# A hybrid decoder step on one core: tensors in the chip's layout, state updates by row strips, two selection rounds a stage, and a later landing time for gathers in the emission clock

## The chip, the cores and the metric

The kernel runs on one core of a Trainium2 chip. The metric is the device time of one launch in microseconds (us). All engines of the core take part: TensorE (PE, its weight loads PEld), VectorE (DVE), ScalarE (ACT), GpSimd (POOL) and SyncE (SP), which issues most of the DMAs.

## What is computed

One inference step of a one-layer hybrid trunk, for a prompt of 256 tokens and 8 sequences of 4 new tokens each (32 tokens), 288 token columns together. The core of the reference:

```python
m = silu(c) @ w_ada + b_ada                     # shift, scale, gate
h = rmsnorm(x, g_norm) * (1 + scale) + shift
(u_a, v_a, z_a, qkv_b, z_b, a_b, b_b, q_c, k_c, v_c, z_c, qi_c, ki_c, wi_c) = split(h @ w_in)
y_a = chunk_mlp(gelu(u_a), layernorm(gelu(v_a))) * silu(z_a)          # a_ws: 128x128 causal mixing
q, k, v = silu(causal_conv(qkv_b, conv_prev, dn_conv_w))              # 4 taps, state_conv
o_b, s_new = gated_delta(l2norm(q), l2norm(k), v, g, beta, state_dn)  # 16 heads of 128x128 states
y_b = rmsnorm(o_b, dn_onorm) * silu(z_b)
idx = top_k(indexer scores, 256 of 2052 keys)                         # 8 sequences, paged caches
y_c = attend(q_c, k[idx], v[idx]) * silu(z_c)
x = x + gate * (concat(y_a, y_b, y_c) @ w_out);  y = rmsnorm(x, g_final)
```

The outputs are y, the new keys, values and index keys, the new delta states, the last pre-convolution rows, and v_a of the new tokens. All data are float32; the large matmuls split each operand into a rounded high part and a low part and use three products.

## The kernel before

**Two kinds of work on PE.** The large matmuls (tile `acc`, 128x288 outputs) are 14304 instructions: unit by unit, one unit being two slices of 128 rows of a weight block, four output tiles and three products each (24 instructions a pair, 12 a slice). For each slice ACT rounds the weights (`wh<-w`), DVE forms the low part (`wl<-w,wh`); four such splits are kept ahead (`N_SPLIT`, line 40). Between these units PE does the small steps of the chains: indexer, top-k selection, sparse attention over gathered keys, convolution, the delta rule (`dn_all`, line 1700), the gMLP part.

**The order is written by an emission clock.** All instructions are recorded in one pass in Python. The class `Weaver` keeps a model time for each engine (`W.t`), adds a table cost for each instruction (`cost`, `note`, `note_dma`), and at each step of the large matmuls asks which chain may go on: `stages` (line 237) steps a generator when its data are ready by the model at PE's model time, and stops where the model's DVE or ACT are over 2 us (`BACKLOG`) ahead of PE. Each `yield` ends a stage of a chain. `bank(n)` waits for n of the four small PSUM banks. So the costs in the table decide where in PE's order a chain step stands, and the engines then run their queues strictly in that order. A DMA's landing in the model is its issue, 0.6 us, its bytes at 360 GB/s, and 2.0 us (line 206); for a DMA issued by POOL (key "G", the gathers) 1.0 us of issue comes on top.

**Forced ends.** `finish` steps named chains to their end at once, with no large matmuls between. Three matter here. Before the last unit of the q columns of head group 2 `end_prev` (line 2285) finishes `DN[0]`, the delta chain of head group 0, and before that of group 3 `DN[1]`. `gmlp_open` (line 2144) finishes `DN[3]`. In counts of large matmuls these places lie at 7752, 8904 and 10992 of the 14304.

**The parts that are touched.**
- Small vectors: `load_rows` and `prep_rows` (line 668) load `b_ada`, `g_norm`, `dn_conv_w` as rows and transpose them on PE (`ldT`, 4 steps); the conditioning vectors `C` are loaded as 72 rows, and transposed (`cT`).
- Convolution: `prev_gen` (line 1589) loads 24 rows of the old convolution state for each of 12 column blocks (`prev`), transposes them (`prevT`, 4 matmuls) and copies them (`scT`). `tail_gen` (line 1631) transposes the new last rows (`tailT`, 4 matmuls), copies them (`tailo`) and stores them with two DMAs.
- Delta states of the 8 sequences: `load_states` (line 1966) and `update` (line 2084) move 512 KB a head, in pieces of 512 B. `update` multiplies, for each head of a group, the keys of that head, which stand on 32 of 128 rows of `kgm` with zeros on the others, with `vk` (tile `Sup`, 128 rows x 512 columns, float32; 8 a group, 32 in all). DVE adds four 128x128 parts of each to the state (`St`).
- Selection: `topk_gen` (line 1350) has 32 rounds on DVE (`MAX8`, `MATCH_REPLACE8` over 544 columns), each a stage of its own, with a copy of the eight found values on POOL (`LDn`).
- Sparse attention of the 32 new tokens: `sample_gen` (line 1432), in two halves of four sequences. In each half two lanes take 16 gathers of keys (`kraw`, 512 KB; transposed as `kT`, multiplied as `S`), the selection's mask is applied, and 16 gathers of values (`vraw`) feed the products `so`. The delta chain of group 0 starts when the second half is done.
- gMLP: `gmlp_prep` (line 2155) loads `a_ws` and transposes it (`wmT`, 8 matmuls).

All instructions bear line 74 in the profile, that of the recording helper; tiles tell them apart.

Of the kernel before, what the change touches and what calls it, by code (L numbers as in the profile page):

```python
# [14 lines left out]
OP = mybir.AluOpType  # L15
# [75 lines left out]
class Weaver:  # L91
# [98 lines left out]
    def note_dma(self, key, out, ins):  # L190
# [15 lines left out]
        self.used(self.parts, out, e + 2.0, "D")  # L206
# [174 lines left out]
def tile_hybrid_step(ctx: ExitStack, tc: tile.TileContext, I, O):  # L381
# [50 lines left out]
    bT = const([P, 96], "bT")  # L432
    gnT = const([P, 32], "gnT")
    cwT = const([P, 4, 48], "cwT")
    onT = const([P, 1], "onT")
# [203 lines left out]
    LD = []  # L639

    def load_rows(dst, src, n):
        t = tl("xp", [P, P], "ld", 4)
        G.dma_start(t[:n], src)
        LD.append((dst, t, n))

    cw = I["dn_conv_w"][0].rearrange("j (c p) -> (j c) p", p=P)
    cwv = cwT.rearrange("p j c -> p (j c)")
    load_rows(bT, I["b_ada"][0].rearrange("(c p) -> c p", p=P), 96)
    load_rows(gnT, I["g_norm"][0].rearrange("(c p) -> c p", p=P), 32)
    load_rows(cwv[:, 0:96], cw[0:96], 96)  # L650
    load_rows(cwv[:, 96:192], cw[96:192], 96)
    G.dma_start(onT, I["dn_onorm"].rearrange("o p -> p o"))

    W.take()
    pc = pr4("cT")
    for h in range(2):
        th = tl("xp", [72, 256], "cth", 1)
        ch = C[:, 256 * h:256 * h + 256]
        A.activation(th, ch, AF.Tanh, scale=0.5)
        V.scalar_tensor_tensor(ch, th, 1.0, ch, op0=OP.add, op1=OP.mult)  # L660
    for c in range(4):
        T.transpose(pc[:, c, 0:72], C[:, c * P:(c + 1) * P], ident[0:72, 0:72])
    A.activation(cT[:, 0:KT * 9].rearrange("p (s c r) -> p c r s", c=4, r=9),
                 pc[:, :, 0:72].rearrange("p c (r s) -> p c r s", s=8), AF.Copy, scale=0.5)
    free()
    load_x(1)

    def prep_rows():
        for dst, t, n in LD:
            yield from bank()  # L670
            ps = pr("ldT")
            T.transpose(ps[:, :n], t[:n, :], ident[:n, :n])
            yield
            V.tensor_copy(dst, ps[:, :n])
            free()
        V.tensor_scalar(onT, onT, 0.5, None, op0=OP.mult)
        yield
# [672 lines left out]
    def topk_gen():  # L1350
# [16 lines left out]
        for n in range(32):  # L1367
            mx = LU[:, 31 - n]
            V.max(out=mx, in_=cur)
            if n < 31:  # L1370
                V.match_replace(out=W1, in_to_replace=mx, in_values=cur, imm_value=-3e38)
            G.tensor_copy(LD_[:, n], mx)
            cur = W1
            yield
# [209 lines left out]
    sconv = I["state_conv"][0].rearrange("b r c -> (b r) c")  # L1584
# [4 lines left out]
    def prev_gen(kind, g):  # L1589
        c0 = kind * 2048 + g * 512  # L1590
        prev = u2k("prev")
        dma2(prev[0:24], sconv[:, c0:c0 + 512])
        yield [prev]
        yield from bank()
        ps = pr4("prevT")
        for j in range(4):
            T.transpose(ps[:, j, 0:24], prev[0:24, j * P:(j + 1) * P], ident[0:24, 0:24])
        yield
        CV[kind, g] = scT = tl("dnq", [P, 4, 24], "scT", 2)
        A.copy(scT, ps[:, :, 0:24])  # L1600
        free()
        yield
# [28 lines left out]
    def tail_gen(kind, g, tail):  # L1631
        c0 = kind * 2048 + g * 512
        yield from bank()
        ps = pr4("tailT")
        for c in range(4):
            T.transpose(ps[0:27, c], tail[:, c], ident)
        yield
        to = u2k("tailo")
        A.copy(to[0:27], ps[0:27].rearrange("p c n -> p (c n)"))
        free()  # L1640
        yield
        dma(O[6][0, 0][:, c0:c0 + 512], to[0:3])
        dma(O[11][0].rearrange("b r c -> (b r) c")[:, c0:c0 + 512], to[3:27])
# [322 lines left out]
    def load_states(g, St):  # L1966
        for hl in range(4):
            yield from W.calm()
            dma2(St[hl], I["state_dn"][0][:, 4 * g + hl].rearrange("b d e -> d b e"))

    def dn_sample(g, b):
# [6 lines left out]
        kgm, vn1, os_, junk = yf(0, 4, P), yf(4, P), yf(5, P), yf(7, P)  # L1978
# [26 lines left out]
        G.memset(kgm, 0.0)  # L2005
# [78 lines left out]
        def update():  # L2084
# [3 lines left out]
            for hl in range(4):  # L2088
                for b0 in (0, 4):
                    yield from bank()  # L2090
# [3 lines left out]
                    for b in range(b0, b0 + 4):  # L2094
                        i = 8 * hl + b
                        V.scalar_tensor_tensor(St[hl][:, b], St[hl][:, b], gl[:, i:i + 1],
                                               pu[:, (b - b0) * P:(b - b0 + 1) * P], op0=OP.mult, op1=OP.add)
                    free()
                yield from W.calm()
                dma(O[10][0, :, 4 * g + hl].rearrange("b d e -> d b e"), St[hl])  # L2100
# [382 lines left out]
```

## Time and profile before

| | |
|---|---|
| median of three runs | 2627.51 us (2625.67 to 2632.01) |
| the profiled execution | 2626.0 us, of which the span from first to last instruction is 2624.3 us |
| busy: PE, PEld | 2509.4 us (96%), 2245.5 us (86%) |
| busy: DVE, ACT, POOL | 1625.4 us (62%), 1065.7 us (41%), 496.1 us (19%) |
| mean granted TensorE clock | 0.986 |
| DMA | 615.9 MB, 235 GB/s over the span |

PE is the engine that sets the time: it is busy nearly always, and a matmul's recorded duration includes the wait in its pipeline, so that what a step costs is read from start to start. "Granted clock" is the share of full speed that TensorE was given; 0.50 is 1.2 GHz, 1.00 is 2.4 GHz.

### The profile page before, as it was taken

What the parts mean: (1) busy time and instruction counts of PE and PEld (TensorE: products, weight loads), DVE (VectorE), ACT (ScalarE), POOL (GpSimd) and SP (SyncE); (2) the same over time, 40 slices, a digit from 0 to 9 for tenths busy, and PEclk for the clock granted to TensorE, in tenths of its full rate; (3) what the DMA queues carried; (4) which work ended last, traced back from release to release, by engine and by line L of the source; (5) the groups of instructions that cost most, each with busy time, mean ns of one, the idle gap of its engine ahead of it and who ended that gap; (6) DMA issues with size and microseconds to landing.
All of it is one profiled execution on the core that took longest, in us unless ns stands there. A gap on an engine that the chain in (4) does not pass through costs nothing.

```text
span 2624.3 us, 52262 instructions
## 1 busy us (share of the span) xinstructions
PE 2509.4 (96%) x19684; PEld 2245.5 (86%) x19684; DVE 1625.4 (62%) x3633; ACT 1065.7 (41%) x2440; POOL 496.1 (19%) x1137
## 2 busy tenths in 40 slices
PE   5999999999998999999999989999999999999997
PEld 3788888888897888878789969989989989999997
DVE  3477765555578786744458567568576667555554
ACT  4423223333344443334354434444444544444443
POOL 2000000000001232353543343343430210000000
PEclk9999999999999999999999999999999999999998
DMA  7999988888665567677777547577568455655565
GB/s 285 365 336 342 338 318 323 310 318 302 206 197 182 186 225 251 220 274 236 246 238 238 176 154 234 184 216 245 184 203 265 146 195 187 187 180 174 174 188 164
DMA packets 234964, 615.91 MB, mean 235 GB/s; under 512 B 38856, under 2 KB 92348, under 8 KB 234712
## 3 DMA queue, kind: packets, MB, share of 16 engines
q1 hardware_dynamic: 223672, 574.65, 64.7%
q0 software_dynamic: 11040, 37.92, 4.3%
q8 instruction: 155, 2.54, 0.4%
q14 instruction: 97, 0.79, 0.1%
HBM read 587.54 MB, written 24.95 MB: 233 GB/s over the span
## 4 chain that ended last, share of the span: by engine, by line
PE 85%; DMA 7%; DVE 3%; POOL 2%; issue 2%; ACT 1%; SPq 0%; ACTq 0%; DVEq 0%; POOLq 0%
PE acc L74 68%; PE ada L74 7%; DMA kraw<-in_cache_k_dram,ixk 2%; DMA wa<-in_w_ada_t_dram 1%; DMA vraw<-in_cache_v_dram,ixv 1%; PE kT L74 1%; DMA w<-in_w_in_t_dram 1%; PE Sup L74 1%; DVE wl L74 1%; PE YP L74 1%; PE v L74 1%; PE gram L74 1%; PE o L74 1%; POOL vraw L74 1%; PE S L74 1%
## 5 line engine op out<-in xcount | busy, mean ns | idle before, releaser
L74 DVE TENSOR_TENSOR wl<-w,wh 128x512 fp32r<-128x512 f32 (+1 forms) x1216 | 802.2, 681 | 687.4 <-ACT wh L74 680.8
L74 ACT CAST wh<-w 128x512 fp32r<-128x512 f32 (+1 forms) x1216 | 715.0, 611 | 1145.5 <-PE acc L74 860.0
L74 PE MATMUL acc<-hH,wh 128*128 128x288 f32 (+1 forms) x3744 | 1157.7, 309 | 21.0 <-ACT hH L74 8.7
L74 PE MATMUL acc<-hH,wl 128*128 128x288 f32 (+1 forms) x3744 | 1110.2, 297 | 2.0 <-DVE wl L74 1.9
L74 PE MATMUL acc<-hL,wh 128*128 128x288 f32 (+1 forms) x3744 | 1110.7, 297 | 0.5 <-DVE hL L74 0.5
L74 PEld LDWEIGHTS acc<-hH,wh 128*128 128x128 f32 (+1 forms) x3744 | 708.8, 189 | 132.5 <-issue 57.6
L74 PEld LDWEIGHTS acc<-hH,wl 128*128 128x128 f32 (+1 forms) x3744 | 709.2, 189 | 4.8 <-DVE wl L74 4.4
L74 PEld LDWEIGHTS acc<-hL,wh 128*128 128x128 f32 (+1 forms) x3744 | 710.1, 190 | 3.6 <-issue 2.4
L74 PE MATMUL acc<-mL,wh 128*128 128x288 f32 x1024 | 301.8, 295 | 2.4 <-DVE mL L74 2.4
L74 PE MATMUL acc<-mH,wh 128*128 128x288 f32 x1024 | 303.5, 296 | 0.0
L74 PE MATMUL acc<-mH,wl 128*128 128x288 f32 x1024 | 302.1, 295 | 0.0
L74 PEld LDWEIGHTS acc<-mL,wh 128*128 128x128 f32 x1024 | 192.2, 188 | 2.7 <-DVE mL L74 2.7
L74 PEld LDWEIGHTS acc<-mH,wh 128*128 128x128 f32 x1024 | 192.2, 188 | 0.2
L74 PEld LDWEIGHTS acc<-mH,wl 128*128 128x128 f32 x1024 | 192.2, 188 | 0.0
L74 PE MATMUL ada<-wa,cT 128*32 128x512 f32 x1024 | 135.7, 605 | 15.8 <-DMA wa<-in_w_ada_t_dram 15.5
L74 DVE TENSOR_TENSOR zb<-zb,acc 128x288 f32<-128x288 f32 x160 | 70.3, 451 | 41.4 <-PE acc L74 41.2
L74 POOL TENSOR_TENSOR htmp<-yT,gaT 128x32 f32<-128x32 f32 x20 | 7.8, 388 | 449.2 <-ACT wh L74 335.4
L74 PEld LDWEIGHTS ada<-wa,cT 128*32 128x32 f32 x1024 | 28.2, 109 | 72.9 <-issue 54.7
L74 POOL TENSOR_SCALAR frs<-frs 128x1 f32<-128x1 f32 (+1 forms) x3 | 0.9, 297 | 448.2 <-DVE frs L74 448.0
L74 DVE TENSOR_TENSOR R<-R,R 128x248 f32<-128x248 f32 (+30 forms) x248 | 72.4, 292 | 11.6 <-DMA R<-dD 5.0
L74 POOL TENSOR_SCALAR tap<-xp,cwT 128x32 f32<-128x32 f32 x144 | 78.5, 545 | 0.2
L74 POOL DMA_INDIRECT vraw<-in_cache_v_dram,ixv x64 | 66.9, 1045 | 31.7 <-issue 12.4
(462 smaller groups left out, 2395.4 us busy)
## 6 DMA issues: line engine op xcount, KB each, us to landing
w<-in_w_in_t_dram SPq DMA_DIRECT2D x464, 512.0 KB
wa<-in_w_ada_t_dram SPq DMA_DIRECT2D x256, 512.0 KB
w<-in_w_ada_t_dram SPq DMA_DIRECT2D x128, 512.0 KB
w<-in_w_out_t_dram SPq DMA_DIRECT2D x128, 512.0 KB
St<-in_state_dn_dram SPq DMA_DIRECT2D x16, 512.0 KB
out_dram<-St SPq DMA_DIRECT2D x16, 512.0 KB
X<-in_x_prompt_dram SPq DMA_DIRECT2D x8, 512.0 KB
XF<-in_x_prompt_dram SPq DMA_DIRECT2D x16, 256.0 KB
```

Source lines behind the costliest of these rows:

```text
L74: r = f(*a, **k)
```

## The change

Inputs and outputs get other layouts in DRAM (`lay_out` and a new `put_back`, on the host): the conditioning vectors, the small vectors (one tile `vecs` instead of four), the convolution state, its new rows, the delta states and `a_ws` come and go as the engines use them. So the transposes `cT`, `ldT`, `prevT`, `tailT` and `wmT` and their copies go (112 matmul entries on PE in the order, 24 copies on ACT), the new convolution rows leave with one DMA a block instead of two, and each partition's part of a delta state is 4 KB in one piece. The update of the states takes the keys of a head from its own 32 rows, two heads side by side, each with a bank. Gathers land 4.0 us instead of 2.0 us after their bytes in the emission clock. The selection has two rounds in a stage, and its copies are on ACT.

```diff
-        self.used(self.parts, out, e + 2.0, "D")
+        self.used(self.parts, out, e + (4.0 if key == "G" else 2.0), "D")
...
-    C = tl("xp", [72, 512], "C")
-    dma(C[0:8], I["c_prompt"].rearrange("r (s c) -> (r s) c", c=512))
-    dma(C[8:72], I["c_sample"].rearrange("r (s c) -> (r s) c", c=512))
+    C = tl("xp", [P, KT * 9], "C")
+    dma(C, I["c_t"])
...
+    dma(vecs, I["vecs_t"])
...
     def prep_rows():
-        for dst, t, n in LD:
...
-            T.transpose(ps[:, :n], t[:n, :], ident[:n, :n])
...
+        yield [vecs]
...
-            G.tensor_copy(LD_[:, n], mx)
+            A.copy(LD_[:, n], mx)
             cur = W1
-            yield
+            if n % 2:
+                yield
...
     def prev_gen(kind, g):
-        c0 = kind * 2048 + g * 512
-        prev = u2k("prev")
-        dma2(prev[0:24], sconv[:, c0:c0 + 512])
-        yield [prev]
...
-            T.transpose(ps[:, j, 0:24], prev[0:24, j * P:(j + 1) * P], ident[0:24, 0:24])
...
+        dma2(scT, I["state_conv_t"][4 * kind + g])
+        yield [scT]
...
     def tail_gen(kind, g, tail):
...
-            T.transpose(ps[0:27, c], tail[:, c], ident)
...
-        dma(O[6][0, 0][:, c0:c0 + 512], to[0:3])
-        dma(O[11][0].rearrange("b r c -> (b r) c")[:, c0:c0 + 512], to[3:27])
+        dma(O[6][4 * kind + g], tail)
+        yield
...
-            dma2(St[hl], I["state_dn"][0][:, 4 * g + hl].rearrange("b d e -> d b e"))
+            dma2(St[hl], I["state_dn_t"][4 * g + hl])
...
-        G.memset(kgm, 0.0)
...
-        for hl in range(4):
-            q = slice(32 * hl, 32 * hl + 32)
-            V.tensor_scalar(kgm[q, hl], pa[q, 1], sc[q, 2:3], None, op0=OP.mult)
+        V.tensor_scalar(kg, pa[:, 1], sc[:, 2:3], None, op0=OP.mult)
...
-            for hl in range(4):
+            for h0 in (0, 2):
                 for b0 in (0, 4):
-                    yield from bank()
-                    pu = pr("Sup")
-                    T.matmul(pu, kgm[:, hl], vk[:, b0:b0 + 4].rearrange("p c n -> p (c n)"), start=True, stop=True)
+                    yield from bank(2)
+                    pus = []
+                    for hl in (h0, h0 + 1):
+                        pus.append(pr("Sup"))
+                        q = slice(32 * hl, 32 * hl + 32)
+                        T.matmul(pus[-1], kg[q], vk[q, b0:b0 + 4].rearrange("p c n -> p (c n)"), start=True, stop=True,
+                                 tile_position=(32 * hl, 0))
                     yield
...
     def gmlp_prep():
-        wraw = tl("gm", [P, 8, P], "wraw", 1)
-        dma(wraw, I["a_ws"][0].rearrange("h t s -> t h s"))
+        wmT = tl("gm", [P, 8, P], "wmT", 1)
+        dma(wmT, I["a_ws_t"])
...
-                T.transpose(ps[:, c], wraw[:, 4 * h4 + c], ident)
```

The order moves from the first selection round on. On DVE, at the start of the selection rounds, before the change (`MAX` and `MATCH_REPLACE` are a round, `wl` a weight split, `ktk` the copy of transposed keys):

```order
L74 MAX LU<-SC 128x8
L74 MATCH_REPLACE W_11002<-LU,SC 128x544
L74 TENSOR_TENSOR wl<-w,wh 128x512
L74 MAX LU<-W_11002 128x8
L74 MATCH_REPLACE W_11002<-LU,W_11002 128x544
L74 TENSOR_TENSOR wl<-w,wh 128x512
L74 COPY ktk<-kT 128x512
L74 MAX LU<-W_11002 128x8
L74 MATCH_REPLACE W_11002<-LU,W_11002 128x544
L74 TENSOR_TENSOR wl<-w,wh 128x512
```

And in the changed kernel, at the same place:

```order
L74 MAX LU<-SC 128x8
L74 MATCH_REPLACE W_10918<-LU,SC 128x544
L74 MAX LU<-W_10918 128x8
L74 MATCH_REPLACE W_10918<-LU,W_10918 128x544
L74 TENSOR_TENSOR wl<-w,wh 128x512 x2
L74 MAX LU<-W_10918 128x8
L74 MATCH_REPLACE W_10918<-LU,W_10918 128x544
L74 MAX LU<-W_10918 128x8
L74 MATCH_REPLACE W_10918<-LU,W_10918 128x544
L74 TENSOR_TENSOR wl<-w,wh 128x512
L74 COPY ktk<-kT 128x512
```

Two rounds now stand together, and from the first to the last of the 32 rounds DVE has 35 splits and 7 copies of keys between them, where it had 42 and 14.

On PE, at the forced end of the delta chain of group 0 (7752 large matmuls into the order), before the change (`osm` and `oTs` are the chain's last steps ahead of the update, `kbT`, `gram` and `qkT` belong to the next group):

```order
L74 MATMUL osm<-R_18134,R_18132 128x128
L74 MATMUL oTs<-ident,R_18134 128x128
L74 MATMUL qkT<-ident,cv 128x128 x8
L74 MATMUL Sup<-R_18396,R_18134 128x512 x3
L74 MATMUL kbT<-ident,R_18379 128x128 x2
L74 MATMUL kbT<-ident,R_18381 128x128 x2
L74 MATMUL gram<-R_18379,cv 128x128
```

And in the changed kernel, from `osm` to the first update:

```order
L74 MATMUL osm<-R_17892,R_17890 128x128
L74 MATMUL acc_17337<-hH_8112,wh 128x288
L74 MATMUL acc_17337<-hL_8126,wh 128x288
L74 MATMUL acc_17337<-hH_8112,wl 128x288
L74 MATMUL qkT<-ident,cv 128x128 x8
L74 MATMUL acc_17306<-hH_8112,wh 128x288
L74 MATMUL acc_17306<-hL_8126,wh 128x288
L74 MATMUL acc_17306<-hH_8112,wl 128x288
```

Before, all steps from `kbT` of the new tokens on, 39 entries, stand at 7752 with no large matmul between them; now the steps up to `osm` stand at 7695 to 7737, among large matmuls, and 22 entries, from `oTs` and four pairs of `Sup` on, are left at 7752. The end of the selection (`cnt`) moves from 5523 to 5316, the last product of the second attention half from 6612 to 6531, the transposes of the delta chain's new tokens (`sT`) of groups 0 to 3 from 7737, 8562, 9657, 10836 to 7668, 8697, 9714, 10860. At 8904, where no chain step stood, 12 entries stand now, two pairs of `Sup` among them.

## Rows read from the trace of the kernel before

**Rows 1.** The page: busy time by engine, and the chain that ended last.

```profile
PE 2509.4 (96%) x19684; PEld 2245.5 (86%) x19684; DVE 1625.4 (62%) x3633; ACT 1065.7 (41%) x2440; POOL 496.1 (19%) x1137
...
PE 85%; DMA 7%; DVE 3%; POOL 2%; issue 2%; ACT 1%; SPq 0%; ACTq 0%; DVEq 0%; POOLq 0%
```

**Rows 2.** The chain in order of time (start us, us, what): large matmuls near the end.

```profile
2252.25 44.15 PE acc L74 x333
```

**Rows 3.** Busy time by stretch, with granted clock (PEclk) and DMA.

```profile
core 0: us, PE busy (x) PEld busy (x) DVE busy (x) ACT busy (x) POOL busy (x), PEclk, DMA share, GB/s
942.90:946.30 3.40, 3.40 (x17) 3.40 (x16) 0.89 (x2) 1.20 (x2) 0.96 (x1) 0.50 0.38 116
1543.70:1547.10 3.40, 3.02 (x8) 1.99 (x9) 0.95 (x5) 1.26 (x5) 1.84 (x8) 0.50 0.00 1
935.00:1075.00 140.00, 132.86 (x1124) 120.48 (x1122) 105.25 (x215) 53.85 (x118) 31.62 (x75) 0.98 0.70 234
1100.00:1300.00 200.00, 185.33 (x1637) 153.53 (x1636) 88.47 (x157) 70.44 (x162) 101.92 (x161) 0.97 0.77 260
1509.40:1548.40 39.00, 27.86 (x220) 17.80 (x220) 20.45 (x76) 14.23 (x65) 14.97 (x44) 0.87 0.25 71
```

**Rows 4.** What PE waited for, 935 to 1075 us (us in total, times, longest).

```profile
PE kT L74 <- DMA kraw<-in_cache_k_dram,ixk: 3.7, 2, 2.3
```

**Rows 5.** The same from 1100 to 1300 us.

```profile
PE so L74 <- DMA vraw<-in_cache_v_dram,ixv: 8.3, 6, 2.5
PE kT L74 <- DMA kraw<-in_cache_k_dram,ixk: 5.7, 3, 3.0
```

**Rows 6.** The page: DMA issues, KB each (of the gathers' indices), median us to landing.

```profile
vraw<-in_cache_v_dram,ixv POOLq DMA_INDIRECT x64, 6.1
...
kraw<-in_cache_k_dram,ixk POOLq DMA_INDIRECT x32, 4.7
```

**Rows 7.** Groups of instructions on PE (busy us, mean ns; idle before).

```profile
L74 PE MATMUL tailT<-ident,tail 128*27 128x128 f32 x48 | 7.3, 274 | 0.0
...
L74 PE MATMUL prevT<-ident,prev 24*128 24x24 f32 x48 | 5.0, 220 | 2.1 <-DMA prev<-in_state_conv_dram 2.1
```

**Rows 8.** PE in order of time (start us, us) around one `prevT`.

```profile
1015.58 0.29 PE L74 MATMUL acc<-hH,wl 128*128 128x288 f32 x1
1015.80 0.43 PE L74 MATMUL prevT<-ident,prev 24*128 24x24 f32 x4
1016.16 0.40 PE L74 MATMUL acc<-hH,wh 128*128 128x288 f32 x1
1016.40 0.29 PE L74 MATMUL acc<-hL,wh 128*128 128x288 f32 x1
```

**Rows 9.** The same around an indexer pair, one `Sup`, and the last group's eight.

```profile
818.34 0.70 PE L74 MATMUL pidx<-ki,v_qi 64*128 64x256 f32 x4
818.97 0.40 PE L74 MATMUL acc<-hH,wh 128*128 128x288 f32 x1
...
1718.51 1.02 PE L74 MATMUL Sup<-R,R 128*128 128x512 f32 x2
...
1719.50 0.29 PE L74 MATMUL acc<-hL,wh 128*128 128x288 f32 x1
...
2133.18 8.73 PE L74 MATMUL Sup<-R,R 128*128 128x512 f32 x16
2141.35 0.69 PE L74 MATMUL acc<-hH,wh 128*128 128x288 f32 x1
```

**Rows 10.** DVE in order of time: the last group's state parts.

```profile
2137.56 6.29 DVE L74 SCALAR_TENSOR_TENSOR St<-St,gls,Sup 128x128 f32<-128x128 f32 x24 [0.59 <-PE Sup L74]
```

**Rows 11.** Groups of instructions on DVE, 900 to 1100 us.

```profile
L74 DVE TENSOR_TENSOR wl<-w,wh 128x512 fp32r<-128x512 f32 x86 | 58.7, 693 | 32.9 <-ACT wh L74 32.2
L74 DVE MAX8 LU<-W 128x8 f32<-128x544 f32 x31 | 22.3, 720 | 0.0
L74 DVE MATCH_REPLACE8 W<-LU,W 128x544 f32<-128x544 f32 x30 | 21.3, 709 | 0.0
```

More of the change, by code (lines that the diff above doesn't have):

```diff
@@ L638, in tile_hybrid_step @@
     load_x(2)
[L639 to L665, printed above, removed]
+    dma(vecs, I["vecs_t"])
+    th = tl("xp", [P, KT * 9], "cth", 1)
+    A.activation(th, C, AF.Tanh, scale=0.5)
+    V.scalar_tensor_tensor(C, th, 1.0, C, op0=OP.add, op1=OP.mult)
+    V.tensor_scalar(cT[:, 0:KT * 9], C, 0.5, None, op0=OP.mult)
     load_x(1)
     def prep_rows():
-        for dst, t, n in LD:
-            yield from bank()
-            ps = pr("ldT")
-            T.transpose(ps[:, :n], t[:n, :], ident[:n, :n])
-            yield
-            V.tensor_copy(dst, ps[:, :n])
-            free()
+        yield [vecs]
         V.tensor_scalar(onT, onT, 0.5, None, op0=OP.mult)
@@ L2087, in update @@
                 V.tensor_scalar(vk[:, b], vn1, bsel[:, b:b + 1], None, op0=OP.mult)
-            for hl in range(4):
+            for h0 in (0, 2):
                 for b0 in (0, 4):
-                    yield from bank()
-                    pu = pr("Sup")
-                    T.matmul(pu, kgm[:, hl], vk[:, b0:b0 + 4].rearrange("p c n -> p (c n)"), start=True, stop=True)
-                    yield
[L2094 to L2100, printed above, removed]
+                    yield from bank(2)
[5 more added lines that the diff above has]
+                                 tile_position=(32 * hl, 0))
+                    yield
+                    for hl, pu in zip((h0, h0 + 1), pus):
+                        for b in range(b0, b0 + 4):
+                            i = 8 * hl + b
+                            V.scalar_tensor_tensor(St[hl][:, b], St[hl][:, b], gl[:, i:i + 1],
+                                                   pu[:, (b - b0) * P:(b - b0 + 1) * P], op0=OP.mult, op1=OP.add)
+                        free()
+                for hl in (h0, h0 + 1):
+                    yield from W.calm()
+                    dma(O[10][4 * g + hl], St[hl])
         MAIN[g] = True
@@ L2161, in gmlp_prep @@
         V.tensor_copy(rep, ident[0:4, None, 0:4].to_broadcast([4, NB, 4]))
-        yield [wraw]
-        wmT = tl("gm", [P, 8, P], "wmT", 1)
-        for h4 in range(2):
-            yield from bank()
-            ps = pr4("wmT")
-            for c in range(4):
-                T.transpose(ps[:, c], wraw[:, 4 * h4 + c], ident)
-            yield
-            V.tensor_tensor(wmT[:, 4 * h4:4 * h4 + 4], ps, K.triI[:, None, :].to_broadcast([P, 4, P]), op=OP.mult)
-            free()
+        yield [wmT]
+        V.tensor_tensor(wmT, wmT, K.triI[:, None, :].to_broadcast([P, 8, P]), op=OP.mult)
+        yield
         yield from bank()
@@ L2461, in lay_out, with put_back @@
     return a
+def put_back(r):
+    r = list(r)
+    conv = r[6].transpose(3, 0, 2, 1).reshape(27, 6144)
+    r[6] = conv[0:3].reshape(1, 1, 3, 6144)
+    r[10] = r[10].transpose(2, 0, 1, 3)[None]
+    r.insert(11, conv[3:27].reshape(1, 8, 3, 6144))
+    return tuple(r)
 def kernel(**inputs):
@@ L2481 @@
     r = _run(nc, [arrays], core_ids=[0])
-    return tuple(r.results[0][f"out_{i}_dram"] for i in range(len(_OUTS)))
+    return put_back([r.results[0][f"out_{i}_dram"] for i in range(len(_OUTS))])
```

41 lines of the change are left out of this document (15 added, 26 removed), and 4 rows, old and new, of the table _OUTS.

## The prediction

> **What bounds the kernel now.** I read the page first, for who is busy and what the chain that ended last is made of. PE is busy 96% of the span, and 85% of the chain is PE's; DMA has 7% [rows 1]. Next the chain in order of time, for the price of the main work: 333 large matmuls follow each other in 44.15 us, 0.1326 us each [rows 2], so a unit's slice of 12 costs 1.59 us, and 14304 of them 1897 us. This part the change leaves alone. What it can win lies in the rest: small steps on PE, waits of PE, and half-speed time of TensorE.
>
> The table by stretch shows both of the last [rows 3]. After a gap in PE's work the granted clock stands at 0.50, the 1.2 GHz level, for some 3.4 us, as from 942.9 and 1543.7 us; there each us of full-speed work takes two, so such a piece costs 1.7 us on top of the gap. From 935 to 1075 us PE is busy 132.86 of 140 us, and DVE, which does the selection, 105.25. From 1100 to 1300 us PE is idle 14.7 us, and a clock of 0.97 over 200 us is some 12 us at half speed, three or four such pieces. From 1509.4 to 1548.4 us, the forced end of the delta chain of group 0, PE is idle 11.1 of 39 us and the clock 0.87, which is 0.13 x 39 = 5.1 us lost.
>
> The list of PE's waits then says for what. From 935 to 1075 it is twice the gathered keys, 3.7 us [rows 4]; from 1100 to 1300 the gathered values, 8.3 us in 6 waits, and keys, 5.7 in 3 [rows 5]. The gathers' row gives the reason: from issue to landing 6.1 us for values and 4.7 for keys, by the median [rows 6], where the emission clock reckons 1.0 + 0.6 + 1.5 (512 KB at 360 GB/s) + 2.0 = 5.1. Half of the values' gathers land later than the order supposes, and PE, running strictly in order, stands still.
>
> **The change, part by part**, against the profiled execution's 2626.0 us (1.5 below the median of 2627.5).
>
> *Transposes removed.* On PE `tailT` takes 7.3 us in all and `prevT` 5.0, with 2.1 of waiting for its rows [rows 7]. `wmT` is 8 steps like those of `tailT`, at 7.3 / 48 = 0.152 us each 1.2. One `prevT` block among large matmuls shows the ends: its step comes 0.22 us after the large matmul ahead of it, where 0.13 is normal, then 0.36 to the next large matmul, and 0.24 to the one behind that, so 0.36 + 0.20 [rows 8]. 12 blocks of 0.56 are 6.7. So 7.3 + 5.0 + 2.1 + 1.2 = 15.6 at least, and, as 12 blocks of `prevT` hold 1.7 more than its busy time and those of `tailT` may pay 0.20 each for their ends, up to 4.1 more. I take **-18** (-13 to -20; the lower end where the removed step had filled one of PE's waits). `cT` and `ldT` stand at the start, where the weights of the conditioning are waited for; 0, within 1.5 either way. The 24 copies on ACT (41% busy) lie beside other work; the single store of the new rows and the states in one piece ask less of DMA. I give them 0: PE waits for neither today. Should the states' load, now 4 KB a partition in one piece, be slower, its lead covers that.
>
> *Updates by strips.* One `Sup` (two instructions) costs 0.86 us: 1718.51 to 1719.50, less one large matmul. The indexer's pair, which already runs on two strips of 64 rows with 256 columns each, took 0.63 from its start to the next large matmul. One after the other they would need half of 0.86 each, 0.86 together; side by side 0.43, and 0.20 for the ends makes 0.63 [rows 9]. So a pair of `Sup` on strips is 0.86 + 0.20 = 1.06 instead of 1.72, an estimate, and four pairs save 2.7 a group. If the strips don't overlap it is 0. That holds where large matmuls surround the pairs, in groups 1 and 2. In group 3, and in what stays forced in group 0, eight `Sup` stand together (8.17 us), and DVE's 32 state parts at 6.29 / 24 = 0.262 us need 8.4 [rows 10]: DVE is the limit with or without strips. So 2 x 2.7: **-5** (0 to -8).
>
> The row of the indexer pair shows that its strips overlap. Of such a switch the Trainium skill says, in "TensorEngine Tiling (Array Packing)", Key Properties, that a change of the tiling mode drains TensorE. By that rule a pair pays on entry and exit; with a further 0.20 a pair this term would be -4 and not -5. No row before the change has strips of 32.
>
> *The forced end of group 0.* 39 steps stand at 7752 with no large matmul between; 22 stay. The lost time is 11.1 + 5.1 = 16.2 us. What stays are the four pairs, limited by DVE to 8.4 us against 4.2 of PE's work: 4.2 lost, and one half-speed piece, 1.7. 16.2 - 5.9 = 10: **-10** (-3 if the steps among the large matmuls only wait elsewhere, -16 at the other end). A new forced piece stands at 8904, with two pairs: 16 parts x 0.262 = 4.2 us against 2.1 of PE, and perhaps a half-speed piece: **+3** (0 to +9; the upper end is a quarter of the 39 us above).
>
> *Gathers at +4.0.* The model's landing becomes 7.1 us, above both medians by 1.0 and 2.4. From 1100 to 1300 us 14.0 us of waits and three pieces of 1.7, so 19.1, are at stake. The longest waits were 2.5 and 3.0 us, where 2.0 is added, so about four waits leave 0.5 to 1 us, too short for a fall of the clock: 4 stay, **-15** (-5 to -19). Later steps need something else to stand there: large matmuls, of which 7700 remain at this point. The lanes' buffers come free later, so the last product moves from 6612 to 6531 only because the selection ended earlier; the delta chain follows it.
>
> *Selection in two rounds a stage.* A round is 0.72 + 0.71 us on DVE, a split 0.69 [rows 11]. Two rounds keep a split waiting 2.9 us, and with the split and ACT's rounding 4.2, against a stock of four splits, 4 x 1.59 = 6.4 us of PE. So a single burst is covered. What decides is the sum: the stage now has 16 slices less on PE. DVE had 105.25 of 140 us; less 16 x 0.69 that is 94, while PE has 132.9 - 16 x 1.59 = 107: DVE at 88%, still below PE, but with little slack for ACT's copies, which wait for each `MAX` in front of the roundings. Gain: the 3.7 us of waiting for keys and 1.7 of half speed, 5.4; loss: I take two or three short waits of PE for a split, 5. **0** (-9 to +10; the upper end is four bursts of 2.9 us that come through).
>
> *The rest.* The whole order behind the selection is shuffled, and any chain step may now wait where it didn't: **+4** (0 to +8), about a tenth of what is gained.
>
> Sum: -18 - 5 - 10 + 3 - 15 + 0 + 4 = -41, so 2585 for a profile like the one before, and 1.5 more for the median: **2586**.
>
> **Rivals.** *First, the selection stage is DVE's.* If the copies on ACT hold up the roundings, DVE's 94 us and its waits outlast PE's 107, and the stage gives back 8 to 16: 2598. For it: DVE at 75% already and 88% after; against it: the average leaves 13 us. *Second, the gathers land later still.* Landing times depend on what else moves (0.77 of the DMA engines' time from 1100 to 1300 us); if the waits shrink only by a third, 5 instead of 15 are won: 2596. *Third, evacuation is the bound.* A pair of `Sup` in 1.06 us gives DVE eight parts, 2.1 us; four banks are all there are, so the next pair waits for the parts and holds PE up in groups 1 and 2 too: the 5 go and 3 are added, 2594. For it speaks that in group 3 the eight took 8.17 us, just DVE's 8.4; against it that large matmuls can fill the time where the order puts them. The Trainium skill states this rule in "TensorEngine Tiling (Array Packing)", PSUM Bottleneck: tiling speeds up TensorE and not the emptying of PSUM, and copies may become the bottleneck. The state parts of group 3 agree, with the 0.262 us above. *Fourth, slower.* Each of the 16 bursts stops PE for its 4.2 us: 67 us at most, less the 41: 2652. The point from which it decides is a stock of splits that never refills, that is DVE at over 100% of PE's time between bursts; at 88% it shouldn't.
>
> **How the numbers follow.** Forecast 0.60, first rival 0.16, second 0.10, third 0.08, fourth 0.03; 0.03 for what I don't see. The first three end below 2612. The terms' bounds, added as if independent, give some 15 us either way; the range is **2562 to 2610**. About 0.3% (7.9 us) is what a measurement can tell from no change: faster, under 2619.6, has all of the forecast and the first three rivals but 0.02: 0.92; same 0.05, slower 0.03.
>
> **What would show it.** Right: no `tailT`, `prevT`, `wmT` in the groups; waits for `vraw` and `kraw` after the selection under 5 us; a clock of 0.99 there; a pair of `Sup` at 1.1 us between large matmuls; the piece at 7752 under 20 us. Wrong: PE waiting for `wl` or `wh` in the selection rounds by more than 10 us (first and fourth rival); waits for gathers over 10 us (second); PE waiting for `St` in groups 1 and 2 (third); or new waits of the delta chains above 8 us in all, which would break the last term.

## The result, and the profile after

The changed kernel takes 2604.34 us (median of 4 runs, 2601.01 to 2608.94) against 2629.76 before (4 runs): a ratio of 0.9905, 95% interval 0.9886 to 0.9925. It is faster, by 25 us; the forecast was 2586, a gain of 41. The time lies in the range of the prediction, near its upper end. The profiled execution has a span of 2600.3 us, 24.0 less than before.

The page of the changed kernel, busy time by engine:

```profile
PE 2498.2 (96%) x19572; PEld 2232.4 (86%) x19572; DVE 1622.6 (62%) x3616; ACT 1055.8 (41%) x2446; POOL 478.0 (18%) x1096
```

PE is as busy as in [rows 1], so as before the question is what stands between its large matmuls. What PE waited for from 900 to 1300 us:

```profile
PE so L74 <- DMA vraw<-in_cache_v_dram,ixv: 3.3, 5, 0.9
PE acc L74 <- DVE zg L74: 0.7, 1, 0.7
PE acc L74 <- ACT wh L74: 0.5, 1, 0.5
PE ptp L74 <- DVE pst L74: 0.5, 1, 0.5
PE kT L74 <- DMA kraw<-in_cache_k_dram,ixk: 0.4, 1, 0.4
PE acc L74 <- DVE wl L74: 0.4, 2, 0.2
```

The 17.7 us of [rows 4, 5] are down to 3.7, and PE waits 0.9 us for splits of weights. The table by stretch of the changed kernel: the 32 selection rounds, the whole stretch of selection and gathers, the forced end of group 0, that at 8904, that of group 3 with the 4 us behind it, and a place near the end:

```profile
core 0: us, PE busy (x) PEld busy (x) DVE busy (x) ACT busy (x) POOL busy (x), PEclk, DMA share, GB/s
919.00:996.10 77.10, 75.51 (x643) 68.00 (x642) 74.15 (x141) 31.24 (x89) 9.50 (x14) 1.00 0.70 234
900.00:1300.00 400.00, 393.40 (x3482) 337.15 (x3471) 255.38 (x499) 164.15 (x417) 161.77 (x286) 1.00 0.75 256
1485.10:1512.30 27.20, 20.31 (x64) 10.55 (x63) 15.85 (x58) 11.23 (x50) 13.14 (x36) 0.72 0.29 106
1718.90:1728.80 9.90, 8.49 (x35) 5.15 (x34) 6.91 (x25) 3.68 (x12) 3.64 (x14) 0.83 0.29 105
2096.20:2111.20 15.00, 11.82 (x36) 6.51 (x35) 11.20 (x44) 0.92 (x3) 1.58 (x4) 0.66 0.49 185
2160.00:2177.00 17.00, 8.71 (x38) 7.71 (x38) 10.79 (x24) 5.88 (x11) 0.00 (x0) 0.70 0.58 199
```

The reader is to see three things. In the rounds themselves DVE is busy 74.15 of 77.1 us, 96%. Up to 1300 us all half-speed time is gone (1.00 where [rows 3] had 0.97 and 0.98). Behind that it is back: 0.72, 0.83, 0.66 and 0.70 in the last four stretches. The last of them stands where PE lost no clock before. It comes from one chain, here in order of time (start us, us, what):

```profile
2160.88 0.63 ACT wh L74
2161.51 0.02 issue
2161.53 0.70 DVE wl L74
2162.24 0.02 issue
2162.25 0.33 SPq L74
2162.58 0.05 issue
2162.63 4.56 DMA mx<-mixD
2167.19 0.02 issue
2167.22 1.16 ACT mH L74
2168.38 0.02 issue
2168.40 1.37 DVE mL L74
```

`mx` is a block of the output product's input (`mix_gen`, in the old file as in the new). Its load stands in SP's queue behind a weight load, which waits for the split that frees its buffer; so it leaves at 2162.6 us, lands at 2167.2, and PE, whose next large matmul needs it, stands still:

```profile
PE acc L74 <- ACT mH L74: 7.5, 1, 7.5
```

To compare kernels whose steps stand at other places, I read from each trace when the large matmuls with certain numbers start. The order is the same up to 4743. From there to 6650 lie selection and attention, to 9300 the forced ends at 7752 and 8904, to 11050 that of group 3, to 11600 the turn to the output product. "At 7752" is the time between the two large matmuls on either side of that place.

| kernel | 4743 to 6650 | 6650 to 9300 | both | at 7752 | at 8904 | 9300 to 11050 | 11050 to 11600 |
|---|---|---|---|---|---|---|---|
| before | 396.2 | 505.6 | 901.8 | 40.2 | 0.1 | 333.0 | 84.2 |
| changed | 374.8 | 493.6 | 868.4 | 27.2 | 9.9 | 333.0 | 92.9 |
| difference | -21.4 | -12.0 | -33.4 | -13.0 | +9.8 | 0.0 | +8.7 |

The differences come to -24.7; up to 4743 and behind 11600 the two traces agree within 0.8 us. One trace is one execution: in the traces of the changed kernel and of the ten kernels made from it below, the part up to 4743, which they share, took between 911.4 and 918.3 us, and in the four of them that share the order from 4743 to 6650 with gathers at 4.0 us that stretch took 374.8 to 381.2. Behind 6650 kernels with the same order agree within 2 us.

### The profile page after: what moved, and what is told of

It is laid out like the page before. It is cut to its first block, busy times and chain, and to the rows that moved or that the text cites. A ratio compares the mean times of both kernels' runs of the same rounds, so it can differ in the third digit from the quotient of the medians.

```text
span 2600.3 us, 51897 instructions
## 1 busy us (share of the span) xinstructions
PE 2498.2 (96%) x19572; PEld 2232.4 (86%) x19572; DVE 1622.6 (62%) x3616; ACT 1055.8 (41%) x2446; POOL 478.0 (18%) x1096
## 5 line engine op out<-in xcount | busy, mean ns | idle before, releaser
L74 POOL DMA_INDIRECT vraw<-in_cache_v_dram,ixv x64 | 66.4, 1038 | 42.1 <-issue 13.9
L74 DVE SCALAR_TENSOR_TENSOR cv<-xp,vecs,cv 128x256 f32<-128x256 f32 x144 | 70.9, 492 | 3.6
```

The costliest lines, as they stand in the source:

```text
L74: r = f(*a, **k)
```

## The experiments

The twelve kernels were timed in three groups of five rounds, each group with the kernel before beside it. A ratio is to that kernel, with its 95% interval behind it; "slower" or "faster than the changed kernel" compares medians of different groups. The kernels named "changed, but" differ from the changed kernel in the edit that is shown, those named "before, with" from the kernel before.

### Undoing single parts

**Full rows for the updates.** The updates use all 128 rows again, with `kgm` cleared and filled as in the kernel before; the order of all steps stays.

```diff
-                        T.matmul(pus[-1], kg[q], vk[q, b0:b0 + 4].rearrange("p c n -> p (c n)"), start=True, stop=True,
-                                 tile_position=(32 * hl, 0))
+                        T.matmul(pus[-1], kgm[:, hl], vk[:, b0:b0 + 4].rearrange("p c n -> p (c n)"), start=True, stop=True)
```

> The changed kernel, with the same order on every engine, but each update of a state is multiplied on all 128 rows again (keys of one head on 32 of them, zeros on the others). Theory (pairs of strips, with no large matmuls among them, leave TensorE at its lower level): the half-speed time at 2101 falls from 10.2 us to 3.4 as in the kernel before, the 17 us at 1490 to 1514 to some 10, and the 3.4 at 1722 goes: 17 us less at half speed are 8.5 saved; a full Sup costs 0.86 us against 0.64 for its half of a pair, times 16 between large matmuls, +3.5; so 5 us faster than the changed kernel. Rival (the gaps alone make the clock fall): half-speed time as in the changed kernel, 3 to 5 us slower than it.

Measured: 2600.25 us, 0.9890 (0.9872 to 0.9908): from the changed kernel not to be told apart by the total. From 6650 to 11050 its trace takes 5.5 us less (488.9 and 332.2), about what the theory said. Of the 10.1 us by which the whole trace is shorter 6.9 lie ahead of 4743, where nothing differs. The stretches tell more (forced ends of group 0, at 8904, of group 3):

```profile
core 0: us, PE busy (x) PEld busy (x) DVE busy (x) ACT busy (x) POOL busy (x), PEclk, DMA share, GB/s
1481.00:1504.60 23.60, 15.81 (x65) 7.89 (x63) 15.64 (x58) 11.14 (x50) 13.12 (x36) 0.93 0.30 106
1711.60:1720.30 8.70, 7.10 (x36) 3.85 (x34) 6.88 (x25) 3.69 (x12) 3.68 (x14) 1.00 0.32 109
2087.70:2097.90 10.20, 7.01 (x21) 3.19 (x19) 8.26 (x33) 0.92 (x3) 1.59 (x4) 1.00 0.45 155
```

The clock stands at 0.93, 1.00 and 1.00 where it was 0.72, 0.83 and 0.66, with the order of the steps unchanged. So strips that stand without large matmuls around them kept TensorE at its 1.2 GHz level for longer here than full rows did. In time that is worth 27.2 - 23.6 = 3.6 us at 7752, 1.2 at 8904 and 1.1 at 10992 (11.2 and 10.1 us between the large matmuls on either side), where 3.2 us of waiting for DVE and DVE's 32 state parts, 8.4 us, make up most of the place either way.

**Landing at 2.0 us again.** In the emission clock, `e + 2.0` for all queues.

> The changed kernel with the gathers' landing time back at 2.0 us in the emission clock. Theory (the later landing removed the waits for gathers and the half-speed pieces behind them): waits for kraw and vraw of 14 to 18 us in all and three to five half-speed pieces of 3.4 us between 900 and 1300 us, so 17 to 25 us slower than the changed kernel. Rival (the shifted order around the selection removed them): waits below 7 us, within 6 us of the changed kernel.

Measured: 2604.76 us, 0.9904 (0.9886 to 0.9921). By the median it is 0.4 us from the changed kernel. The rival has the time right and the waits wrong (13.4 us, not under 7); the theory has the waits nearly right and the time wrong. Its mechanism is there, in the waits of PE from 900 to 1300 us and in the clock; but the forced end is gone as well (second stretch):

```profile
PE so L74 <- DMA vraw<-in_cache_v_dram,ixv: 7.8, 6, 1.8
PE kT L74 <- DMA kraw<-in_cache_k_dram,ixk: 5.6, 4, 2.5
```

```profile
core 0: us, PE busy (x) PEld busy (x) DVE busy (x) ACT busy (x) POOL busy (x), PEclk, DMA share, GB/s
900.00:1300.00 400.00, 375.98 (x3253) 317.29 (x3245) 238.47 (x462) 148.04 (x375) 148.17 (x255) 0.97 0.72 241
1500.00:1535.00 35.00, 34.31 (x240) 28.02 (x239) 23.67 (x70) 17.86 (x61) 13.02 (x37) 1.00 0.65 213
```

From 4743 to 6650 it takes 406.0 us, 31.2 more than the changed kernel, and from 6650 to 9300 472.1, 21.5 less: at 7752 and 8904 0.1 us each. The traced execution is the slowest of the five, 6.5 us above their median, so the difference of 9.7 is an upper figure. With landing at 2.0 the delta chain of group 0 starts 165 large matmuls earlier in the order (7503 instead of 7668) and ends before it is forced.

**One round a stage again.** In `topk_gen` the `if n % 2:` ahead of `yield` goes.

> The changed kernel with one round of the selection in a stage again (its copies stay on ACT). Theory of the prediction (the two rounds give and take nothing): within 4 us of the changed kernel, with PE waiting for splits for under 3 us more or less between 900 and 1070 us. Rival (two rounds a stage leave PE waiting behind DVE): 8 to 16 us faster than the changed kernel. Second rival (the earlier end of the selection is what let the gathers land in time): 5 to 15 us slower, with waits for vraw or kraw over 5 us.

Measured: 2612.76 us, 0.9939 (0.9921 to 0.9957), some 8 us slower than the changed kernel, and as far as the second rival said, but for another reason: PE waits 1.0 us for `vraw` and none for `kraw`. The selection ends at 5466 instead of 5316, and the delta chain, which comes last, pays at its forced end:

```profile
1472.40:1518.30 45.90, 34.39 (x217) 20.61 (x216) 20.17 (x77) 16.21 (x71) 16.36 (x46) 0.65 0.23 80
```

45.9 us instead of 27.2, with 124 steps instead of 41.

### Single parts of the change in the kernel before

**Before, with landing at 4.0 us.**

```diff
-        self.used(self.parts, out, e + 2.0, "D")
+        self.used(self.parts, out, e + (4.0 if key == "G" else 2.0), "D")
```

> The kernel before, with one edit of the change: gathers land 4.0 us after their bytes in the emission clock. In its order 128 steps stand at the forced end of group 0 (125 before). Theory (two terms that pull against each other: later landings remove the gathers' waits, and start the delta chain later, so that its end is forced): waits for kraw and vraw below 5 us where they were 17.7, and at most one half-speed piece between 900 and 1300 us where there were five, 20 to 26 us won there; the forced piece stays at 37 to 45 us; so 2602 to 2612. Rival (the gathers land still later when they are issued elsewhere): waits over 10 us and 2618 or more.

Measured: 2621.17 us, 0.9970 (0.9956 to 0.9984). The direction of each stage came as the theory had it (16.2 us less from 4743 to 6650; 4.5 more from 6650 to 9300), but the gain is less than what it said (20 to 26 in the first), and the run lies 9 us above its bound. From 900 to 1300 us 10.2 us at half speed are left of 17.1, where the theory allowed 3.4. The waits from 900 to 1300 us show new ones beside the shorter gathers, `prevT` above all:

```profile
PE prevT L74 <- DMA prev<-in_state_conv_dram: 4.4, 1, 4.4
PE so L74 <- DMA vraw<-in_cache_v_dram,ixv: 3.8, 3, 1.9
PE mask L74 <- DVE mneg L74: 2.2, 1, 2.2
PE acc L74 <- DVE wl L74: 2.0, 3, 1.7
```

And from 11050 to 11600 it takes 4.8 us more than before (89.0). The forced end:

```profile
1491.70:1536.20 44.50, 30.90 (x225) 19.17 (x224) 21.90 (x82) 15.89 (x71) 17.05 (x49) 0.77 0.29 80
```

**Before, with two rounds a stage** (and the copies on ACT).

```diff
-            G.tensor_copy(LD_[:, n], mx)
+            A.copy(LD_[:, n], mx)
             cur = W1
-            yield
+            if n % 2:
+                yield
```

> The kernel before, with one edit of the change: two selection rounds in a stage, with the copies on ACT. In its order no step is left at the forced end of group 0. Theory (what two rounds bring is that the selection takes fewer slices of large matmuls, so the attention and the delta chain start earlier): the piece of 39 us at 7752 goes, of which 27.9 were PE's work at 0.87 of the clock, so 12 to 18 us are won there; the gathers' waits stay, 14 to 20 us with three to six half-speed pieces; in the selection itself nothing is won or lost by more than 4 us; so 2610 to 2618. Rival (the selection stage becomes DVE's and gives back 8 to 16): 2621 or more, with PE waiting over 6 us for splits between 900 and 1060 us.

Measured: 2604.54 us, 0.9914 (0.9894 to 0.9935). This one edit is worth what the whole change is. The gathers' waits stay, 13.9 us from 900 to 1300:

```profile
PE so L74 <- DMA vraw<-in_cache_v_dram,ixv: 9.4, 6, 2.8
PE kT L74 <- DMA kraw<-in_cache_k_dram,ixk: 4.5, 3, 2.3
```

4743 to 6650 takes 398.2 us (+2.0), 6650 to 9300 480.5 (-25.1), and the place at 7752 0.1 instead of 40.2. I had reckoned 12 to 18 us for it, so the run lies 5 us below my range. The rival falls: PE waited for no split from 930 to 1060 us. What the copies on ACT do without the second round was not run in this kernel.

**The layouts alone.** The changed kernel with landing at 2.0, one round a stage with copies on POOL, and the updates of the kernel before.

> The changed kernel with only its layouts left: gathers at 2.0 us, one selection round a stage with copies on POOL, updates on all 128 rows one by one. Theory (the transposes are worth some 10 us on PE from start to start, not 18, and the order gives part of it back): tailT, prevT and wmT go, -10; in this order 84 steps stand at the forced end of group 3 (9 before), which by the forced end of group 0 (125 steps, 16 us lost) loses some 8 to 12 us; gathers' waits and the forced end of group 0 stay as before; so 2622 to 2632, within 0.3% of the kernel before. Rival (the prediction's term holds): 2608 to 2614.

Measured: 2630.94 us, 1.0008 (0.9993 to 1.0022): no change. Up to 9300 it gains 9.2 us (393.1 and 499.5), and from 9300 to 11050 it loses 10.3, at the forced end of group 3, 27.1 us where there were 10.7:

```profile
2109.90:2136.90 27.00, 18.57 (x163) 11.04 (x163) 12.52 (x51) 3.95 (x16) 4.72 (x15) 0.81 0.20 70
```

Another 2.7 are lost from 11050 to 11600. That the changed order has only 9 steps there, as before, is due to its other parts.

### The new wait, and a better version

**Changed, but the blocks loaded in order.** The order on SP had the fourth block ahead of the third.

```diff
     def mix_gen(kb):
         yield lambda: hasattr(X, "gm")
+        yield lambda: MXN[0] == KB.index(kb)
...
         dma2(mx, mixD[kb])
+        MXN[0] += 1
```

> The changed kernel, but the loads of the four delta blocks for the output product (mx) are issued strictly in the order in which PE needs them (blocks 2, 3, 4, 5 instead of 2, 3, 5, 4); otherwise the order on PE differs only by four groups of mix. Theory (the swap makes PE wait): the wait of 7.5 us for mH at 2160.9 goes, and with it the half-speed piece of 10.2 us behind it, which cost 5.1; 0 to 3 us of waiting stay as in the kernel before, so 9 to 12 us faster than the changed kernel, some 2593. Rival (the load is late whatever its place, since SP's queue waits for the weights' buffers): the wait moves to the next block, within 3 us of the changed kernel.

Measured: 2601.36 us, 0.9898 (0.9879 to 0.9917); from 11050 to 11600 90.5 us instead of 92.9. So the swap cost 2.4 us at most and is not the main cause: in either order the load is late, and PE still waits 5.4 us for the blocks in this trace (8.3 in the changed kernel).

**Changed, but without the wait ahead of these loads.**

```diff
-        yield from W.calm()
         dma2(mx, mixD[kb])
```

> The changed kernel, but the loads of the four delta blocks for the output product (mx) no longer wait until the model's DMA clock is near PE's; its third stands 9 weight loads further ahead in SP's queue (606 instead of 615). Theory (in the changed order these loads stand too far behind the weight loads in SP's queue): the wait of 7.5 us for mH at 2161 and the half-speed piece of 10.2 us behind it go, 8 to 12 us faster than the changed kernel in that stretch, some 2593. Rival (the wait is for the engines that round the block, not for its load): it stays within 2 us of 7.5, and the time within 3 us of the changed kernel's.

Measured: 2592.90 us, 0.9864 (0.9842 to 0.9886). From 11050 to 11600 it takes 81.1 us, 11.8 less than the changed kernel, and PE waits for no block; the stretch is full:

```profile
2145.00:2170.00 25.00, 25.00 (x186) 24.35 (x185) 22.54 (x47) 12.29 (x24) 0.00 (x0) 1.00 0.57 173
```

SP issues the fourth load at 2126.7 us instead of 2162.6. `calm` holds a load back while the model's DMA clock is over 2.5 us ahead of PE's; here that put it behind weight loads which wait for PE.

**Changed, but landing at 3.5 us.** In its order the last attention product stands at 6438 (6531 with 4.0) and the delta chain of group 0 starts at 7503, as with 2.0.

> The changed kernel with the gathers' landing at 3.5 us instead of 4.0. In its order the forced end of group 0 is empty, as with 2.0, and the 20 steps at 8904 are gone. Theory (4.0 pays for its safety with the forced end; 3.5 lies above the gathers' median of 6.1 us by half a us and starts the delta chain in time): the forced pieces go, 20 to 27 us; of the gathers' waits 2 to 8 us come back with one or two half-speed pieces; so 12 to 22 us faster than the changed kernel, 2582 to 2592. Rival (waits return as with 2.0): 15 to 20 us of waits, and no faster than the changed kernel.

Measured: 2587.58 us, 0.9844 (0.9824 to 0.9864), 17 us faster than the changed kernel. 4743 to 6650 takes 384.1 us (9.3 more), 6650 to 9300 474.3 (19.3 less). Of the waits those for values are 6.7 us, with 3.3 at 4.0 us; those for keys are gone:

```profile
PE so L74 <- DMA vraw<-in_cache_v_dram,ixv: 6.7, 7, 1.6
```

**Both of these edits.**

> The changed kernel with two edits that each gained alone: landing at 3.5 us, and the loads of mx without the wait for the model's DMA clock. If the two are independent: 2588 - 12 = 2576, within 4 us; the half-speed piece of 13.7 us at 10992 stays. If one only moved what the other meets, 2584 or more.

Measured: 2578.69 us, 0.9797 (0.9772 to 0.9821). They add: the sum was 2576, within 4.

**Both, with full rows.**

> The same two edits, and all updates on 128 rows instead of strips, in the same order. Theory (strips pay among large matmuls, 0.22 us a Sup, 24 of them, and cost half-speed time where they stand alone, 13.7 us in group 3): -6 in group 3, +5 in the others, so within 3 us of the run with strips. Rival (full rows cost nothing among large matmuls either): 5 to 7 us faster.

Measured: 2576.80 us, 0.9797 (0.9774 to 0.9820), not to be told apart from strips, as the theory had it. Its `Sup` take 4.6 us more in all, counted from start to start; from 9300 to 11050 it needs 334.2 us, with strips 334.0.

**Both, with full rows in group 3 alone.**

> The same two edits, strips in groups 0 to 2 and 128 rows in group 3 alone, in the same order. Theory: it has both gains, the half-speed piece at 10992 at most 3.4 us, so 5 to 7 us faster than the run with strips everywhere, some 2570, and 3 to 5 faster than that with full rows everywhere. Rival (the lower level there is not for the strips): no faster than strips everywhere.

Measured: 2574.61 us, 0.9787 (0.9762 to 0.9811), the lowest median of all, though not by more than the intervals allow. The half-speed piece at 10992 was 6.8 us long instead of 13.7, so in the first row below, of this kernel, the clock is higher than in the second, of that with strips everywhere, and yet the place takes no less time:

```profile
2083.20:2096.30 13.10, 9.91 (x21) 4.29 (x19) 9.00 (x35) 0.92 (x3) 1.59 (x4) 0.74 0.39 136
```

```profile
2088.50:2100.80 12.30, 9.12 (x20) 3.38 (x18) 9.13 (x36) 0.92 (x3) 1.58 (x4) 0.65 0.44 156
```

The place is 3.2 us of waiting for DVE at its start, then DVE's 32 parts, 8.4 us, which with full rows at the lower clock also had to wait for `Sup`. The expected 5 us of gain there do not exist; what the two traces differ by lies elsewhere, from 4743 to 6650 (383.5 and 388.8), where the two kernels have the same order.

## Why the prediction came out as it did

Set side by side, the two parts that act on the order explain the result:

| kernel | landing, rounds a stage | 4743 to 6650 | 6650 to 9300 | both |
|---|---|---|---|---|
| before | 2.0, one | 396.2 | 505.6 | 901.8 |
| before, landing | 4.0, one | 380.0 | 510.1 | 890.1 |
| before, rounds | 2.0, two | 398.2 | 480.5 | 878.7 |
| changed, one round | 4.0, one | 363.0 | 516.5 | 879.5 |
| changed, landing | 2.0, two | 406.0 | 472.1 | 878.1 |
| changed | 4.0, two | 374.8 | 493.6 | 868.4 |
| changed, landing | 3.5, two | 384.1 | 474.3 | 858.4 |

Attention steps move over the border between the two columns, so the sum is what counts. Two rounds are worth 23.1 us in the kernel before and 11.1 in the changed one; the later landing 11.7 and 9.7. By the medians of the runs it is 24 and 8 for two rounds, 7 and under 1 for the landing: between 2.0 and 4.0 us in the changed kernel no gain is shown. Two rounds make the selection end earlier and so empty the forced end of group 0 in the kernel before; the later landing removes the gathers' waits, and by starting the delta chain later fills that forced end again. At 4.0 us it fills it with 41 steps and adds 20 at 8904; at 3.5 it fills nothing.

The prediction priced two kinds of things: PE's work, and time that PE loses. For the second its measure was PE's idle time plus half of the time at half speed. Here that measure is read for whole stretches, with the forecast's terms put where their steps stand (7, 14 and 3 of the 24 transposed blocks, a group of strips in each of the second and third stretches):

| us, before to changed | 4743 to 6650 | 6650 to 9300 | 9300 to 11050 | 11050 to 11600 | all |
|---|---|---|---|---|---|
| PE idle | 21.9 to 5.5 | 15.2 to 10.5 | 2.2 to 4.2 | 2.4 to 8.3 | |
| at half speed | 17.1 to 0 | 10.2 to 20.5 | 3.4 to 10.2 | 0 to 10.2 | |
| lost, difference | -25.0 | +0.4 | +5.4 | +11.0 | -8.2 |
| lost, forecast | -15 | -7 | 0 | +4 | -18 |
| the rest, difference | +3.6 | -12.4 | -5.4 | -2.3 | -16.5 |
| the rest, forecast | -5 | -12.5 | -5 | -1 | -23 |

So the time lies in the range partly by luck: the gathers' stretch won 10 us more than was forecast, while the forced ends, the strips' clock and the new wait took 20 more, and PE's work fell by 6 less. "Lost" is an upper figure where PE, at half speed, would have waited for DVE or ACT anyway.

By the prediction's steps:

- *Gathers at +4.0, -15, and selection, 0: the mechanism is right, the sum too small.* The waits fell from 17.7 to 3.7 and no half-speed time is left up to 1300 us. At stake were 17.7 us of waits and five half-speed pieces, 1.7 each; nearly all of it went. The prediction let 4 us stay, and set against the 5.4 it saw ahead of 1100 us a loss of 5 that did not come. That waits under 1 us are too short for a fall of the clock held in this run (longest 0.9, clock 1.00); with landing at 2.0 a half-speed piece of 6.8 us (from 1208.9) came behind one of 0.9. Of the +3.6 of other work part is steps that stood behind 6650 before: PE has 1316 small instructions there as before, though the 28 of seven blocks are gone. What the step left out is its price behind: with 2.0 the forced ends would have been empty (21.5 us less from 6650 to 9300).
- *The slack of DVE: smaller than was worked out.* The prediction had DVE at 88% with 16 slices less on PE. The order shows 7 splits less between the rounds, not 16, and in the rounds DVE is busy 96%. That PE waited only 0.9 us for splits shows the four splits kept ahead were enough, with little to spare. The worth of this edit lies 500 us later, at the forced end, where the prediction had it under another name.
- *Forced end of group 0, -10: the step that failed most.* The place is 13.0 us shorter, but it has 41 steps instead of 125, and those that left it cost PE's work elsewhere. By the prediction's own measure 16.2 us were lost before; now it is 6.9 of idle time and 0.28 x 27.2 = 7.6 of clock, 14.5. So the term was worth -2, not -10. What stays was priced at 5.9, as four pairs limited by DVE and one half-speed piece. The runs show PE waiting 3.8 us for the chain's `oTs` ahead of the pairs, and 15.5 us at half speed; with full rows that is 3.4, though only 3.6 us of time come back. That the loss hardly shrank other runs show too: from 6650 to 9300 the kernel before gained 25.1 us when its place was emptied (two rounds), and the changed kernel still has 21.5 to gain (landing at 2.0). The prediction's own sign, a piece under 20 us at 7752, was missed with 27.2.
- *New place at 8904, +3: right in size, for another reason.* By the same measure it lost 1.4 of idle time and 0.17 x 9.9 = 1.7 of clock. DVE's state parts did not hold PE up there (DVE is busy 6.91 of 9.9 us); PE waited four times for ACT.
- *Transposes, -18: too large, and not to be had alone.* The prediction took `tailT` by its busy time, 7.3 / 12 = 0.61 a block, and added 0.20 for the ends. From start to start a block alone among large matmuls costs 0.35 to the next large matmul and 0.09 behind that, 0.44 (kernel before):

```profile
1419.65 0.29 PE L74 MATMUL acc<-hH,wl 128*128 128x288 f32 x1
1419.78 0.60 PE L74 MATMUL tailT<-ident,tail 128*27 128x128 f32 x4
1420.13 0.38 PE L74 MATMUL acc<-hH,wh 128*128 128x288 f32 x1
1420.35 0.29 PE L74 MATMUL acc<-hL,wh 128*128 128x288 f32 x1
```

So 12 x 0.44 for `tailT`, 6.7 for `prevT`, 0.9 for `wmT` and 2.1 of waits make 15.0. Of that some 12.7 lie ahead of 9300; the layouts alone saved 9.2 there, and the forced end of group 3 took 10.3 back. The likely reason is that the chains need the same time by the emission clock: when steps of PE go, that time covers more large matmuls, and more of a chain is left when its end is forced (84 steps at 10992 instead of 9).
- *Strips, -5: small.* In the changed kernel a pair among large matmuls, from PE's rows in order of time:

```profile
1896.33 0.29 PE L74 MATMUL acc<-hH,wl 128*128 128x288 f32 x1
1896.55 1.13 PE L74 MATMUL Sup<-R,R 32*128 32x512 f32 x4
1897.61 0.40 PE L74 MATMUL acc<-hH,wh 128*128 128x288 f32 x1
1897.85 0.30 PE L74 MATMUL acc<-hL,wh 128*128 128x288 f32 x1
```

and the same two heads on full rows, in the run with landing at 3.5 and full rows:

```profile
1671.05 0.29 PE L74 MATMUL acc<-hH,wl 128*128 128x288 f32 x1
1671.18 1.88 PE L2049 MATMUL Sup<-R,R 128*128 128x512 f32 x4
1672.49 0.70 PE L74 MATMUL acc<-hH,wh 128*128 128x288 f32 x1
```

The pair takes 1.06 us to the next large matmul, as estimated from [rows 9], and 0.09 ahead of it and 0.11 behind it on top: 1.26 instead of 1.06. On full rows it starts 0.13 behind the large matmul, as the next large matmul would, and costs 1.71 in all. So four pairs save 4 x (1.72 - 1.26) = 1.8 us, not 2.7. The Trainium skill's rule that a change of the tiling mode drains TensorE ("TensorEngine Tiling (Array Packing)", Key Properties) was given there with 0.20 a pair; the trace agrees, with these 0.20 us, which full rows do not pay. And where the strips stand alone, they cost clock, as the run with full rows showed; "DVE is the limit with or without strips" left that out. In group 3 the half-speed piece reaches 3.8 us past the place, which costs 1.9, and the place takes 0.5 more; with that the 2.4 that came elsewhere from 9300 to 11050 are gone.
- *The rest, +4: too small, for a cause of another kind.* Not a step of a chain but a load made PE wait: the new wait for `mH` and its half-speed piece made +8.7 from 11050 to 11600; the run without `calm` took 11.8 away there.

Of the rivals none came: PE waited 0.9 us for splits (first and fourth, though DVE was closer to its limit than was thought), the gathers landed in time (second), and PE did not stand still for the state parts in groups 1 and 2 (third; what it waited for them at the forced ends was 1.1 us).

The prediction spoke of the order of all edits together; the order of each edit alone would have shown which of them fills or empties a forced end.

Open stays why, in the changed order, `calm` holds the loads of `mx` back longer than before; the model's DMA clock at that place was not read out. Why landing at 4.0 in the kernel before won only half of what was expected is shown in its new waits and the 10.2 us left at half speed, but not taken apart. Why the layouts alone saved 9.2 us where single blocks add up to 12.7 is open too. Landings between 3.5 and 4.0, and below 3.5 with the other edits, were not run.

## What to carry to other kernels

Where a table of costs writes the order, an edit pays at two places: where its wait was, and at the next place where a chain is forced to end; price both, and find out from the order of each edit alone how many steps are left there. A safe estimate for a transfer's landing is not free: with two rounds a stage, 4.0 us instead of 3.5 saved 9 us of waits and cost 19 in two forced ends. What a forced end loses is its idle time and its clock, not its length: steps that move out of it still cost their work. Short steps that are taken off the engine that is always busy bring little by themselves if the chains beside it wait for their latencies.

## What the runs showed of the hardware that I had not expected

Matmuls on strips of 32 rows, two side by side, went with TensorE at 1.2 GHz for longer where they stand in a row: at the forced end of group 3 the half-speed piece was 10.2 to 13.7 us long in the seven traces with strips in that place, and 0 to 6.8 in the six with full rows and the same nine steps. Against full rows it cost the changed kernel 1.1 us in the place, and about 1.9 behind it. What in the strips does it was not tested.

Two heads on strips side by side take 1.26 us with their ends, on full rows one behind the other 1.71, and one head alone on full rows 0.86 ([rows 9]). So running them side by side saves 0.45 us of the 0.86 that full overlap without ends would save.
